# Two norm sums and three PSUM bank orders at the passages of a two-layer backbone

## The chip, the cores and the metric

One core of a Trainium2 chip runs the whole kernel as one program. The metric is the device time of one execution in microseconds (us). Work is spread over five engines that run side by side, each through its own list of instructions in a fixed order: PE (matrix products), DVE (vector engine), ACT (scalar engine), POOL (GpSimd) and SP, which issues the DMAs. An instruction starts when those ahead of it on its engine have gone and the semaphores that it waits for are up.

## The reference, cut to what matters

Two layers work on 640 tokens of width 1024 (128 context tokens and 512 latent ones). Each layer has a mixer (layer 0: mLSTM and HGRN2, layer 1: differential attention) and a SwiGLU feed-forward (FFN). Both add their result to the residual stream x, and each reads x through a norm with a modulation:

```
def _rmsnorm(x, g):
    xf = x.astype(f32)
    return xf * lax.rsqrt(jnp.mean(xf * xf, axis=-1, keepdims=True) + EPS) * g.astype(f32)
```

So each of these passages needs, for every token, the sum over the 1024 channels of x squared, its inverse root r, and x times r times a scale plus a shift. A final norm follows the last layer. All of it is in fp32. A large product is made as three, from a rounded high part and a low part of either operand.

## The kernel before, in words

x lies in SBUF with channels on partitions: eight tiles (k = 0 to 7) of 128 channels, each with 640 tokens in two halves of 320 (HALF; a = 0 and 1). There are three **passages** in the middle, all written by `transition` (L534), and one at the end, `to_output`: T01 from the mixer of layer 0 to its FFN (about 478 to 524 us of the span), T10 from that FFN to the attention (968 to 1020 us), T11 from the attention to the last FFN (1338 to 1390 us), and the output (from 1796 us).

A passage runs thus. The last products of the stage before are added to x, half 0 first, one k after the other (`add_x`, L370, on DVE). `sq_sum` (L480) squares the eight tiles of that half on ACT (L488); POOL adds the squares k = 1 to 5 into `sq` (L490); the squares k = 6 (`s2`) and k = 7 stay as they are, so that the sum is handed on in three parts. `columns` (L549) lets PE add over channels: five groups of 64 tokens, three matmuls with one column each, for the three parts; then DVE adds EPS (`r`, L554), POOL takes the power -1/2 (L555) and DVE spreads r on a diagonal (`dg`, L557). `spread` (L560) multiplies `dg` by ones on PE, so that a PSUM bank `rs` holds r for all partitions. DVE multiplies x by `rs` (L503, tile `hf`), ACT and DVE modulate (L511, L513), the high part `hh` is a cast (L519) and the low part `hl` a subtraction (L525); in these chains the order on DVE is pinned. The adds to x of half 1 run beside this, with `sq_sum` for half 1. `BEFORE` says behind which product of half 1 `columns` and `spread` of half 0 are written.

Then `switch` releases the PSUM banks of the old stage, allocates those of the new, and returns `first`, which makes the first products of the new stage from half 0 (`proj_open`): for T01 and T11 (`to_ffn`) the products u and v and then a second u, for T10 (`to_odd`) two products of q and k and then one of v. `BEHIND` says behind which k of these products PE does `columns` and `spread` for half 1. PE keeps program order within a passage; on the other engines and in the FFN stages a scheduler sets it.

`sq_sum`'s second adds, POOL's own additions of FFN weights (L1283 to L1286) and the power L555 share POOL's list. At T10 a one-row piece of the attention's parameters comes by DMA (`lp`, issued at L1537), and DVE multiplies it at L1540.

In the output, `sq_sum` is called for each half, and `chunk` uses the parts for 128 tokens at a time: means on PE, then transposes and a scaling on DVE and ACT, then the DMA out.

Of the kernel before, what the change touches and what calls it, by code (L numbers as in the profile page):

```python
# [163 lines left out]
def hybrid_kernel(ctx: ExitStack, tc: tile.TileContext, A: dict, O: dict):  # L164
# [316 lines left out]
    def sq_sum(pool, a):  # L481

        t = slice(a * HALF, (a + 1) * HALF)
        sq = pool.tile([P, HALF], F32, tag="nsq", name="sq", bufs=2)
        s2 = pool.tile([P, HALF], F32, tag="ns2", name="s2", bufs=1)
        for k in range(KD):
            dst = {0: sq, SQUARES: s2}.get(k) or pool.tile([P, HALF], F32, tag="ns1", name="s1", bufs=2)
            S.activation(dst, x[:, k, t], AF.Square)  # L488
            if 0 < k < SQUARES:
                G.tensor_tensor(sq, sq, dst, op=ALU.add)  # L490
        return sq, s2, dst

    def norm_out(pool, l, which, a, rs, ks=range(KD), keep=None):

# [44 lines left out]
    def transition(l, which, add, tag0, switch, tag1, nada, ada_bank, extra=0):  # L539
# [7 lines left out]
        def columns(sq, tag):  # L547

            o = bank(tag)  # L549
            for i in range(NC64):  # L550
                for j, part in enumerate(sq):
                    T.matmul(o[0:64, i:i + 1], lhsT=part[:, i * 64:(i + 1) * 64], rhs=mean1, start=j == 0, stop=j == 2)
            r = pool.tile([64, NC64], F32, tag="nr", name="r", bufs=2)
            V.tensor_scalar(r, o[0:64, 0:NC64], EPS, None, op0=ALU.add)  # L554
            G.tensor_tensor(r, r, mhalf[0:64, 0:NC64], op=ALU.pow)  # L555
            dg = pool.tile([64, NC64, 64], F32, tag="ndg", name="dg", bufs=1)
            V.tensor_tensor(dg, ident[0:64, 0:64].unsqueeze(1).to_broadcast([64, NC64, 64]),  # L557
                            r.unsqueeze(2).to_broadcast([64, NC64, 64]), op=ALU.mult)
            return dg
# [774 lines left out]
    def ffn_open(l, behind):  # L1334
# [7 lines left out]
        with tc.issue_after(behind):  # L1342
            w2 = w_cols(A["ffn_w1"][l], P)

        def first(a, between):
            (u, v), t = proj_open(ws, a, between)
            ffn_up(st, 0, u, t)
            ffn_gate(st, 0, v, t)
            ffn_act(st, 0, t)
            (u,), t = proj_open([w2], a, lambda k: between(k + KD))  # L1350
            ffn_up(st, 1, u, t)

        def rest():
# [138 lines left out]
    def to_odd(behind):  # L1492
        ff["st"]["wide"].release()
        ff["st"]["pool"].release()
        psum["p"].release()
        psum_pool(pj=2, s=2, p1=2)
        ff["od"] = tc.alloc_tile_pool(name="od", bufs=1, reuse_waits="tile")
        qk[0] = at_tiles()
        ws = [w_cols(w_in1, j * D, "r") for j in range(2)]
        with tc.issue_after(behind):  # L1500
            wv = w_cols(w_in1, 2 * D)
        ff["vt"] = vt_tile()

        def first(a, between):
            os, t = proj_open(ws, a, between)
            for j in range(2):
                at_evac(j, qk[0][j], a, os[j], t)
            (o,), t = proj_open([wv], a, lambda k: between(k + KD), [bank("s", 2)[:, 0:HALF]])
            S.copy(ff["vt"][:, t], o)

        return first
# [262 lines left out]
    def to_output():  # L1774
        ff["st"]["wide"].release()
        with tc.tile_pool(name="fi", bufs=1, reuse_waits="tile") as fi:
# [13 lines left out]
            def chunk(c):  # L1790
                o = bank("nm")
                for a in range(2):
                    t0, t1 = max(c * P, a * HALF), min((c + 1) * P, (a + 1) * HALF)
                    if t0 < t1:
                        for j, part in enumerate(sqs[a]):
                            T.matmul(o[t0 - c * P:t1 - c * P, 0:1], lhsT=part[:, t0 - a * HALF:t1 - a * HALF],
                                     rhs=mean1, start=j == 0, stop=j == 2)
                V.tensor_scalar(rcol[:, c:c + 1], o[:, 0:1], EPS, None, op0=ALU.add)
                G.tensor_tensor(rcol[:, c:c + 1], rcol[:, c:c + 1], mhalf[:, 0:1], op=ALU.pow)
                for b in range(2):  # L1800
# [58 lines left out]
```

## Time and profile before

| | us |
|---|---|
| median of 3 runs (1825.88 to 1830.09) | 1828.68 |
| the profiled execution | 1829.14 |
| its span in the trace | 1827.4 |
| PE busy in the span | 1751.1 (96%) |
| DVE busy | 1338.0 (73%) |
| ACT busy | 767.4 (42%) |
| POOL busy | 434.2 (24%) |

The span is what the trace covers; the 1.7 us between it and the execution's own time lie around it. In rows of the timeline the first number is the start in us from the span's start, the second the duration of the row (of all its instructions, where it ends in x2 or more), and in square brackets stands how long the engine was idle just before, and who ended that. `nm`, `p`, `pj` and `s` are PSUM tiles, `raw` and `own` are weights as they come in.

### The profile page before, as it was taken

Reading aid. Unit: us, or ns where it says so; the run is one execution under the profiler, and the core shown is the slowest. Engines: PE = TensorE matmul, PEld = TensorE weight load, DVE = VectorE, ACT = ScalarE, POOL = GpSimd, SP = SyncE. Lnnn points to the kernel's source line nnn. Section 1 sums busy time; section 2 is a strip of 40 time slices with the busy share of each in tenths; the row PEclk is TensorE's granted clock in tenths of the full one; section 3 lists DMA queues with packets and bytes.
Section 4 is the critical chain, followed back from the end, with each engine's and each line's share of the span. In section 5 each row is a group of like instructions: output and inputs, shape, how many; then the busy total and the mean of one; then the engine's idle time right before and its main releaser. Section 6 shows DMA issues by size and latency. Waiting matters only on the chain.

```text
span 1827.4 us, 31939 instructions
## 1 busy us (share of the span) xinstructions
PE 1751.1 (96%) x12446; PEld 1673.6 (92%) x12446; DVE 1338.0 (73%) x2778; ACT 767.4 (42%) x1617; POOL 434.2 (24%) x373
## 2 busy tenths in 40 slices
PE   7999999999888999999999899999989999999998
PEld 5788999998778999999998898999978999999998
DVE  5645775668687777777777678667869887887876
ACT  5434343333352333333334466566635333333334
POOL 2100012223313222222212221112131423332312
PEclk9999999999989999999999999999999999999999
DMA  9255222123515344444313121012031322223211
GB/s 310 90 153 169 77 64 64 51 72 99 165 48 172 115 151 127 139 128 136 107 56 101 40 88 44 28 54 76 28 116 58 93 82 81 82 81 93 70 58 58
DMA packets 191818, 174.80 MB, mean 96 GB/s; under 512 B 7506, under 2 KB 176308, under 8 KB 191668
## 3 DMA queue, kind: packets, MB, share of 16 engines
q1 hardware_dynamic: 190404, 172.62, 30.7%
q8 instruction: 99, 1.62, 0.4%
q14 instruction: 51, 0.42, 0.1%
q10 hardware_dynamic: 1264, 0.14, 0.1%
HBM read 167.99 MB, written 4.74 MB: 95 GB/s over the span
## 4 chain that ended last, share of the span: by engine, by line
PE 80%; DVE 11%; ACT 3%; issue 2%; DMA 2%; POOL 1%; ACTq 0%; SPq 0%; POOLq 0%; DVEq 0%
PE pj L187 61%; PE nm L187 8%; PE p L187 6%; PE s L187 2%; DVE wl L318 2%; PE p L192 1%; DVE x L370 1%; ACT wh L317 1%; DVE hl L525 1%; PE pj L192 1%; DMA raw<-in_ffn_w_dram 1%; DVE hh L519 1%; DMA wg<-in_ev_w_in_dram 0%; DVE e L1662 0%; DVE t L1259 0%
## 5 line engine op out<-in xcount | busy, mean ns | idle before, releaser
L187 PE MATMUL pj<-hh,wh 128*128 128x320 f32 x1648 | 526.8, 322 | 20.0 <-DVE hf L503 9.3
L187 PE MATMUL pj<-hh,wl 128*128 128x320 f32 x1648 | 513.7, 312 | 0.6 <-DVE wl L318 0.6
L187 PE MATMUL pj<-hl,wh 128*128 128x320 f32 x1648 | 502.1, 312 | 2.1 <-DVE hl L525 1.9
L187 PEld LDWEIGHTS pj<-hh,wh 128*128 128x128 f32 x1648 | 313.7, 191 | 34.4 <-DVE hf L503 9.6
L187 PEld LDWEIGHTS pj<-hh,wl 128*128 128x128 f32 x1648 | 313.7, 190 | 1.0 <-DVE wl L318 1.0
L187 PEld LDWEIGHTS pj<-hl,wh 128*128 128x128 f32 x1648 | 310.0, 190 | 4.3 <-DVE hl L525 2.4
L187 PE MATMUL pj<-t,wh 128*128 128x320 f32 x960 | 215.8, 310 | 0.0
L317 ACT CAST wh<-raw 128x1024 fp32r<-128x1024 f32 x127 | 132.8, 1050 | 193.1 <-PE pj L187 89.3
L318 DVE TENSOR_TENSOR wl<-raw,wh 128x1024 fp32r<-128x1024 f32 x127 | 158.8, 1252 | 54.0 <-ACT wh L317 44.0
L187 PEld LDWEIGHTS pj<-t,wh 128*128 128x128 f32 x960 | 160.4, 188 | 2.1 <-DVE o L1321 0.8
L187 PE MATMUL pj<-t,wl 128*128 128x320 f32 x480 | 148.4, 309 | 1.5 <-DVE wl L1270 1.5
L1269 ACT CAST wh<-s 128x1024 fp32r<-128x1024 f32 x80 | 84.1, 1051 | 153.1 <-PE pj L187 153.0
L1283 POOL TENSOR_TENSOR s<-raw 128x512 f32<-128x512 f32 x40 | 56.0, 1399 | 331.4 <-DVE wl L1270 317.7
L370 DVE SCALAR_TENSOR_TENSOR x<-nm,g2h,x 128x128 f32<-128x128 f32 (+1 forms) x236 | 93.5, 429 | 49.2 <-PE nm L187 49.0
L370 DVE SCALAR_TENSOR_TENSOR x<-pj,g2h,x 128x128 f32<-128x128 f32 (+2 forms) x292 | 112.0, 431 | 16.2 <-PE pj L187 15.6
L187 PE MATMUL pj<-ah,wh 128*128 128x320 f32 x392 | 122.9, 313 | 0.0
L187 PE MATMUL pj<-al,wh 128*128 128x320 f32 x392 | 121.5, 310 | 0.0
L187 PE MATMUL pj<-ah,wl 128*128 128x320 f32 x392 | 121.4, 310 | 0.0
L1285 POOL TENSOR_TENSOR s<-s,raw 128x512 f32<-128x512 f32 x40 | 67.1, 1678 | 195.7 <-DVE wl L1270 173.3
L1270 DVE TENSOR_TENSOR wl<-s,wh 128x1024 fp32r<-128x1024 f32 x80 | 97.2, 1215 | 8.8 <-ACT wh L1269 8.7
L1269 ACT CAST wh<-raw 128x512 fp32r<-128x512 f32 (+1 forms) x81 | 67.9, 838 | 78.0 <-PE pj L187 77.9
L187 PE MATMUL nm<-al,wh 128*128 128x320 f32 x312 | 95.8, 309 | 1.6 <-DVE al L1385 1.6
(411 smaller groups left out, 3795.4 us busy)
## 6 DMA issues: line engine op xcount, KB each, us to landing
raw<-in_ffn_w_dram SPq DMA_DIRECT2D x132, 512.0 KB
own<-in_ada_w_dram SPq DMA_DIRECT2D x48, 512.0 KB
raw<-in_ev_w_in_dram SPq DMA_DIRECT2D x36, 512.0 KB
raw<-in_ada_w_dram SPq DMA_DIRECT2D x36, 512.0 KB
raw<-in_od_w_in_dram SPq DMA_DIRECT2D x24, 512.0 KB
araw<-in_ada_w_dram SPq DMA_DIRECT2D x12, 512.0 KB
raw<-in_ev_w_out_dram SPq DMA_DIRECT2D x8, 512.0 KB
raw<-in_od_w_out_dram SPq DMA_DIRECT2D x8, 512.0 KB
```

Source lines behind the costliest of these rows:

```text
L187: ins = nc.tensor.matmul(*args, **kw)
L192: ins = nc.tensor.transpose(*args, **kw)
L317: S.copy(wh, raw3)
L318: V.tensor_tensor(wl, raw3, wh.bitcast(F32), op=ALU.subtract)
L370: V.scalar_tensor_tensor(x[:, m, t0:t1], o[:, t0 - a * HALF:t1 - a * HALF], gate[:, m, c:c + 1], x[:, m, t0:t1], op0=ALU.mult, op1=ALU.add)
L519: order(V.tensor_copy(hh[:, k, t], tmps[k]))
L525: order(V.tensor_tensor(hl[:, k, t], tmps[k], hh[:, k, t].bitcast(F32), op=ALU.subtract))
L1269: S.copy(wh, src)
L1270: V.tensor_tensor(wl, src, wh.bitcast(F32), op=ALU.subtract)
L1283: G.tensor_tensor(sa[:, 0], a21, a22, op=ALU.add)
L1285: G.tensor_tensor(sb[:, 0], sa[:, 0], a11, op=ALU.subtract)
```

## The change

`sq_sum` returns one sum. For half 0, POOL still adds k = 1 to 5, and DVE adds k = 7 to `s2` and `s2` to `sq`. For half 1 all seven adds are DVE's. `columns` and `chunk` then have one matmul for a group of tokens in place of three. In `to_ffn` three banks are allocated ahead and handed to the products of half 0 in another order, (1, 2, 0) for layer 0 and (0, 2, 1) for layer 1; in `to_odd` both `s` banks are allocated ahead of the first products.

```diff
@@ sq_sum
             if 0 < k < SQUARES:
-                G.tensor_tensor(sq, sq, dst, op=ALU.add)
-        return sq, s2, dst
+                (V if a else G).tensor_tensor(sq, sq, dst, op=ALU.add)
+            elif k > SQUARES:
+                V.tensor_tensor(s2, s2, dst, op=ALU.add)
+        V.tensor_tensor(sq, sq, s2, op=ALU.add)
+        return sq
@@ columns
-                for j, part in enumerate(sq):
-                    T.matmul(o[0:64, i:i + 1], lhsT=part[:, i * 64:(i + 1) * 64], rhs=mean1, start=j == 0, stop=j == 2)
+                T.matmul(o[0:64, i:i + 1], lhsT=sq[:, i * 64:(i + 1) * 64], rhs=mean1, start=True, stop=True)
@@ to_ffn
+        os = [pj()[:, 0:HALF] for _ in range(3)]
+        os = [os[i] for i in ((1, 2, 0), (0, 2, 1))[l]]
+
         def first(a, between):
-            (u, v), t = proj_open(ws, a, between)
+            (u, v), t = proj_open(ws, a, between, None if a else os[0:2])
...
-            (u,), t = proj_open([w2], a, lambda k: between(k + KD))
+            (u,), t = proj_open([w2], a, lambda k: between(k + KD), None if a else os[2:])
@@ to_odd
+        vs = [bank("s", 2)[:, 0:HALF] for _ in range(2)]
+
...
-            (o,), t = proj_open([wv], a, lambda k: between(k + KD), [bank("s", 2)[:, 0:HALF]])
+            (o,), t = proj_open([wv], a, lambda k: between(k + KD), [vs[a]])
@@ chunk
-                        for j, part in enumerate(sqs[a]):
-                            T.matmul(o[t0 - c * P:t1 - c * P, 0:1], lhsT=part[:, t0 - a * HALF:t1 - a * HALF],
-                                     rhs=mean1, start=j == 0, stop=j == 2)
+                        T.matmul(o[t0 - c * P:t1 - c * P, 0:1], lhsT=sqs[a][:, t0 - a * HALF:t1 - a * HALF],
+                                 rhs=mean1, start=True, stop=True)
```

In the listings below the line numbers of the changed kernel are 2 to 8 higher; a number behind a name tells tiles of one name apart.

DVE at T01, from `r` of half 0 to its first three multiplications by `rs`; `x` is an add to the residual of half 1, `adar` and `g2h` belong to the modulation of a later stage. Before:

```order
L554 TENSOR_SCALAR r<-pj 64x5
L370 SCALAR_TENSOR_TENSOR x<-pj,mod,x 128x320 x2
L453 TENSOR_REDUCE adar<-p_5372 128x4
L557 TENSOR_TENSOR dg<-ident,r 64x320
L471 TENSOR_TENSOR g2h<-adar,v_123 128x4
L370 SCALAR_TENSOR_TENSOR x<-pj,mod,x 128x320
L472 TENSOR_SCALAR g2h<-g2h 128x4
L503 TENSOR_TENSOR hf<-x,pj 128x320 x3
```

Now:

```order
L556 TENSOR_SCALAR r<-pj 64x5
L490 TENSOR_TENSOR sq<-sq,s_5528 128x320
L370 SCALAR_TENSOR_TENSOR x<-pj,mod,x 128x320 x2
L453 TENSOR_REDUCE adar<-p_5374 128x4
L490 TENSOR_TENSOR sq<-sq,s_5531 128x320
L471 TENSOR_TENSOR g2h<-adar,v_123 128x4
L559 TENSOR_TENSOR dg<-ident,r 64x320
L370 SCALAR_TENSOR_TENSOR x<-pj,mod,x 128x320
L490 TENSOR_TENSOR sq<-sq,s_5534 128x320
L472 TENSOR_SCALAR g2h<-g2h 128x4
L506 TENSOR_TENSOR hf<-x,pj 128x320 x3
```

Three adds for half 1 now stand among these rows, and `g2h` stands ahead of `dg`; four more adds stand outside of the piece, one of them ahead of it.

POOL at the same place, from the last add of half 0 to the power for half 1. Before:

```order
L490 TENSOR_TENSOR sq<-sq,s_5533 128x320
L1284 TENSOR_TENSOR s<-raw 128x512
L490 TENSOR_TENSOR sq<-sq,s_5536 128x320
L555 TENSOR_TENSOR r<-r,mhalf 64x5
L1283 TENSOR_TENSOR s<-raw 128x512
L490 TENSOR_TENSOR sq<-sq,s_5539 128x320
L1285 TENSOR_TENSOR s<-s,raw 128x512
L490 TENSOR_TENSOR sq<-sq,s_5542 128x320
L1286 TENSOR_TENSOR s<-raw,s 128x512
```

Now:

```order
L1286 TENSOR_TENSOR s<-raw 128x512
L557 TENSOR_TENSOR r<-r,mhalf 64x5
L1285 TENSOR_TENSOR s<-raw 128x512
L1287 TENSOR_TENSOR s<-s,raw 128x512
L1288 TENSOR_TENSOR s<-raw,s 128x512
```

The adds of half 1 are gone from POOL's list; one of them stood ahead of the power. The four weight sums stay, in the same order.

DVE at the end of T10, from the next to last `wl` (low part of a weight) to `dg` of half 1. Before:

```order
L318 TENSOR_TENSOR wl<-raw,wh 128x1024
L525 TENSOR_TENSOR hl<-hf,hh 128x320
L1540 TENSOR_TENSOR l_11044<-lp 1x128
L1542 TENSOR_REDUCE ls<-l_11044 1x2
L554 TENSOR_SCALAR r<-p_10854 64x5
L1545 SCALAR_TENSOR_TENSOR nl<-ls 1x1
L557 TENSOR_TENSOR dg<-ident,r 64x320
```

Now:

```order
L318 TENSOR_TENSOR wl<-raw,wh 128x1024 x2
L528 TENSOR_TENSOR hl<-hf,hh 128x320
L492 TENSOR_TENSOR s_10744<-s_10744,s_10762 128x320
L528 TENSOR_TENSOR hl<-hf,hh 128x320
L493 TENSOR_TENSOR sq<-sq,s_10744 128x320
L556 TENSOR_SCALAR r<-p_10834 64x5
L1548 TENSOR_TENSOR l_11012<-lp 1x128
L559 TENSOR_TENSOR dg<-ident,r 64x320
```

The last two adds of half 1 stand ahead of `r`; `r` has moved ahead of the instruction that waits for `lp`, and `dg` stands right behind that one.

## Rows read from the trace of the kernel before

**Rows 1.** Windows: busy us and count of PE, PEld, DVE, ACT, POOL; granted clock.

```profile
508.60:512.80 4.20, 4.20 (x16) 4.20 (x17) 3.29 (x8) 1.16 (x2) 0.00 (x0) 0.50 0.16 25
512.90:515.30 2.40, 2.40 (x18) 2.29 (x16) 0.00 (x0) 0.00 (x0) 0.00 (x0) 1.00 0.43 166
```

**Rows 2.** Timeline of PE at T01: start, duration, form, idle time before.

```profile
489.70 0.28 PE L187 MATMUL pj<-mean,sq 128*64 128x1 f32 x2
...
491.54 0.41 PE L187 MATMUL pj<-hh,wh 128*128 128x320 f32 x1
...
496.37 0.77 PE L187 MATMUL pj<-dg,ones 64*128 64x320 f32 x2 [1.70 <-DVE dg L557]
...
508.59 0.63 PE L187 MATMUL pj<-hh,wh 128*128 128x320 f32 x1 [9.31 <-DVE hf L503]
```

**Rows 3.** Timeline of DVE at T01.

```profile
494.67 1.55 DVE L557 TENSOR_TENSOR dg<-ident,r 64x320 f32<-64x320 f32 x1 [0.43 <-POOL r L555]
496.15 2.05 DVE L471 TENSOR_TENSOR g2h<-adar,v 128x4 f32<-128x4 f32 x1
...
498.58 1.68 DVE L472 TENSOR_SCALAR g2h<-g2h 128x4 f32<-128x4 f32 x1
500.18 1.27 DVE L503 TENSOR_TENSOR hf<-x,pj 128x320 f32<-128x320 f32 x3
...
501.91 0.14 DVE L471 TENSOR_TENSOR g2h<-adar,v 128x4 f32<-128x4 f32 x1
```

**Rows 4.** Timeline of POOL at T01.

```profile
492.64 0.87 POOL L490 TENSOR_TENSOR sq<-sq,s 128x320 f32<-128x320 f32 x1
493.47 1.17 POOL L555 TENSOR_TENSOR r<-r,mhalf 64x5 f32<-64x5 f32 x1
494.62 1.25 POOL L1283 TENSOR_TENSOR s<-raw 128x512 f32<-128x512 f32 x1
...
496.90 1.27 POOL L1285 TENSOR_TENSOR s<-s,raw 128x512 f32<-128x512 f32 x1
```

**Rows 5.** One line each: count, duration in ns (least, median, most).

```profile
L490 POOL TENSOR_TENSOR sq<-sq,s x40: 851/876/1100, 482.4 to 1814.8; 128x320 f32<-128x320 f32 x40
```

```profile
L525 DVE TENSOR_TENSOR hl<-hf,hh x24: 473/483/789, 503.0 to 1378.8; 128x320 fp32r<-128x320 f32 x24
```

**Rows 6.** Timeline of PE in the first FFN.

```profile
564.62 0.64 PE L187 MATMUL pj<-own,cpad 128*32 128x256 f32 x8 [2.41 <-DMA own<-in_ada_w_dram]
```

**Rows 7.** Timeline of DVE at T10.

```profile
989.04 1.55 DVE L513 TENSOR_SCALAR hf<-hf,amod,mod 128x128 f32<-128x128 f32 x2
...
996.77 0.63 DVE L513 TENSOR_SCALAR hf<-hf,amod,mod 128x128 f32<-128x128 f32 x2
...
1000.63 0.48 DVE L525 TENSOR_TENSOR hl<-hf,hh 128x320 fp32r<-128x320 f32 x1
1006.29 0.28 DVE L1540 TENSOR_TENSOR l<-lp 1x128 f32<-1x128 f32 x1 [5.18 <-DMA lp<-in_od_lambda_dram]
...
1008.24 0.48 DVE L557 TENSOR_TENSOR dg<-ident,r 64x320 f32<-64x320 f32 x1 [0.94 <-POOL r L555]
```

**Rows 8.** Timeline of PE at T10.

```profile
993.84 0.41 PE L187 MATMUL pj<-hh,wh 128*128 128x320 f32 x1 [3.14 <-DVE x L370]
...
1008.78 1.43 PE L187 MATMUL p<-dg,ones 64*128 64x320 f32 x2 [4.36 <-DVE dg L557]
```

**Rows 9.** Timeline of SP's DMA issues at T10.

```profile
1001.78 0.28 SPq L1537 DMA_DIRECT2D lp<-in_od_lambda_dram  x1
```

**Rows 10.** Timeline of DVE at T11.

```profile
1362.13 1.69 DVE L471 TENSOR_TENSOR g2h<-adar,v 128x4 f32<-128x4 f32 x1
```

**Rows 11.** Timeline of PE at T11.

```profile
1365.14 0.80 PE L187 MATMUL p<-dg,ones 64*128 64x320 f32 x2 [2.62 <-DVE dg L557]
```

**Rows 12.** Timeline of ACT and DVE in the output.

```profile
1815.64 0.82 ACT L488 ACTIVATE s<-x 128x320 f32<-128x320 f32 x2
...
1817.34 0.16 DVE L1798 TENSOR_SCALAR rcol<-nm 128x1 f32<-128x1 f32 x1 [1.86 <-PE nm L187]
```

## The prediction

> **What bounds the kernel now.** I read the page's busy times first, which stand in the table ahead: PE is busy for 96% of the span, so over most of it the time is PE's, and an engine beside it has room. Then the timeline of PE at the three passages and in the output, since there PE stands idle, and each idle time names its releaser. At T01 the columns of half 0 take PE from 489.70 to the next product at 491.54, 1.84 us for fifteen column matmuls (the profile has two records for each); PE then waits 1.70 us for `dg`, makes `rs`, and waits 9.31 us for the first product of the FFN until the last `hf` multiplication [rows 2]. Behind that wait its granted clock is 0.50, 1.2 GHz of 2.4, for 4.2 us in which 16 matmuls were made, against 18 in the next 2.4 us at full clock [rows 1]. Third, the timelines of DVE and POOL at the same place: between `dg` and the first `hf` DVE does little, yet `dg` takes 1.55 us and two operations on 128x4 take 2.05 and 1.68 us, where the same one took 0.14 us at 501.91 [rows 3]; POOL meanwhile goes through its adds, the power and its weight sums without a pause [rows 4]. At T10 PE waits 3.14 us for an add to x and later 4.36 us for `dg` of half 1 [rows 8], which comes behind the landing of `lp` on DVE [rows 7]. At T11 it waits 2.62 us for `dg` [rows 11]. So at the passages the time is set by one chain: columns, r, power, `dg`, spread, `hf`, then the chain on DVE.
>
> **The prices.** An add of the change on POOL has a median of 0.876 us, and twenty go [rows 5]. DVE gains nine adds at each of four places, 36. None of this form is in the trace on DVE; its nearest row is `hl`, the same 128x320 with both inputs in SBUF, with a median of 0.483 us [rows 5]; in an unbroken run, as in the three `hf` that take 1.27 us [rows 3], one costs 0.40 us. I take 0.40 on a chain. As bounds an add costs nothing, where DVE waits anyway, and 1.25 us more where a POOL weight sum of that length holds it up [rows 4]. Of each column place two thirds of the matmuls go: 1.84 x 2/3 = 1.2 us of PE [rows 2].
>
> **T01.** Three things. (1) Half 0: the columns are 1.2 us shorter, so r comes that much earlier. The power no longer stands behind an add (492.64 to 493.51 [rows 4]), but still behind the weight sum that ends where that add began, so it gains only about 0.8 us and ends near 493.85. `dg` then either starts at once or behind L1283, which follows on POOL directly and would end at 495.1; it ended at 496.22, so it gains 0.6 to 1.8 us. Of the two stalled `g2h`, which cost 3.4 us beyond their own length, part goes with two POOL adds in this stretch. I take `hf` to begin 1.5 us earlier than 500.18, from bounds of 0.7 and 2.3. (2) Behind that start three adds (k = 5, k = 7, and the last) stand in the chain that ends with the `hf` for which PE waits: 3 x 0.40 = +1.2. (3) Columns of half 1: -1.2 on PE, which runs without a pause there. Sum -1.5, from -3 to -0.3 by the bounds.
>
> The new order of banks gives nothing here. In the built program the spread of half 0 and the first product stand in the same PSUM bank with either order, so that the first product goes on waiting for the last `hf`, and the 9.31 us only shrink with the chain.
>
> **The FFN behind it.** The scheduler puts some products of the first FFN in another order; the second four of a group on `own` now stand about a dozen matmuls behind the first four, where before eight waited 2.41 us for the DMA [rows 6]. If all were hidden: -2.4; if the wait only moves, or another comes in: 0 to +1. I take -0.5, since a later FFN product may run into the same load.
>
> **T10.** The columns of half 0 give 1.2 us to `rs`. POOL's adds, which stalled the chain, are gone: the modulation took 1.55 us where its like took 0.63 [rows 7], the longest `hl` 0.79 for 0.48 [rows 5], so -1.2 at least. Against it stand six of seven adds ahead of the last `hl`, 6 x 0.40 = +2.4. The last `hl`, at 1000.63 [rows 7], stays where it was, or within a microsecond of it. `lp` is issued behind that, at 1001.78 [rows 9], and DVE takes it at 1006.29 [rows 7], 4.5 us later; I leave this as it is. What is gained is behind it: from the start of the `lp` multiplication to the start of `dg` there were 1.95 us (1008.24 - 1006.29), since r stood behind it and the power behind r; now r is made while `lp` is on its way, and `dg` starts 0.28 us behind. -1.7, and with a last `hl` 0.4 us earlier -2.1. The seventh add stands behind the last `hl`, in the time in which DVE waits for `lp`, so it costs nothing; if that cover went it would be 0.4. Bounds: -3.3 (a last `hl` 1.6 earlier), -0.6 (1.1 later, as the full +2.4 without stalls removed). The wait of 3.14 us goes with the banks, as the first products no longer stand in the bank of the last add to x; but PE only reaches the `hh` casts sooner, and later waits for `dg` as before. I book nothing for it.
>
> **T11.** `dg` stood behind a `g2h` that took 1.69 us [rows 10]. Now r is 1.2 us earlier, POOL's last weight sum starts earlier too, and three adds more stand ahead of `dg`: 2.62 us of waiting [rows 11] become about 1.7, and `rs` comes some 2.1 us earlier. One add then hides under the wait for the spread, two stay in the chain, and I charge a third for holds: +1.2. Columns of half 1: -1.2. Sum -2.1, from -3.5 to 0.
>
> **The output.** The last two squares end at 1816.46, and DVE took the mean at 1817.34 [rows 12]. Two adds, 0.97 us, now stand between: +0.5 for that chunk, as its mean needs fewer matmuls. The two chunks behind it lose four column matmuls each, 4 x 0.12 = 0.5 a chunk. Net -0.4, from -1.5 to +1.5.
>
> **A rule.** Operations of DVE with both inputs in SBUF were long only while POOL was at work: `dg` and `g2h` [rows 3] against POOL's run [rows 4]. The Trainium skill, "SBUF — State Buffer", section "Who interferes with whom", says that a VectorE instruction with two inputs in SBUF contends with a GpSimd instruction that reads SBUF, and that the one that comes first holds the shared ports for its whole length. The trace agrees. By that rule each of the 36 new adds can be held up, and holds up POOL in turn, which speaks against the change: it puts more such instructions on DVE where the weight sums remain.
>
> **The rivals.**
> (a) **Cover only, no change.** T01's `hf` does not start earlier, since the weight sums take the place of POOL's adds: +1.2 - 1.2 = 0. T10 gives the 1.7 behind `lp`. T11 gives its columns less one hold, -0.4, the output -0.4, the FFN nothing: -2.5, 1826.6. For it: POOL has the same four weight sums in the same order. Against it: POOL loses four adds in the same stretch.
> (b) **Slower: the adds are held.** The mechanism is DVE's adds of half 1 waiting for POOL's weight sums and lengthening the chain. T01: +1.2, one hold of 1.25, columns -1.2: +1.3. T10, where POOL has no weight sum, only the adds: +2.8 on the last `hl` and `lp`, less 1.7: +1.1. T11 as T01: +1.3. Output: +0.9 with no column gained back. Sum +4.6, 1833.7. It decides from the point where T01's first `hf` starts no earlier than 500.2 and T10's last `hl` over 1.7 us later than 1000.63. Against it: the stalls at T10 were made by the adds that go. This is where the rule above leads if DVE loses each race.
> (c) **The banks do act at T01**: the first product starts when `hh` is there. PE would then make products while DVE works; some 25 of the matmuls that follow the wait would be made in it, at 0.13 us (2.40 / 18 [rows 1]) 3.3 us: 1819.2. Against it: the placement in the built program.
> (d) **The slow clock goes with the waits.** 16 matmuls took 4.20 us at 0.50 where 18 took 2.40 [rows 1], so this stretch alone is worth 2.1 us; with a second one at T10 or T11 of this size, -4.2 beyond the forecast: 1818.3. Against it: the long waits shrink by 1 to 2 us only.
>
> **How the numbers follow.** The sum: -1.5 - 0.5 - 2.1 - 2.1 - 0.4 = -6.6. The profiled execution took 1829.14 us, 0.46 above the median of 1828.68 and inside the runs' own range: 1829.14 - 6.6 = 1822.5. Chances: forecast 0.44 (1819.5 to 1825), (a) 0.30, (b) 0.10, (c) 0.06, (d) 0.10. 0.2%, about what a measurement of this kernel can tell from no change, is 3.7 us: faster is below 1825.0, slower above 1832.3. The forecast, (c) and (d) are faster, (a) is the same, (b) is slower: 0.60, 0.30, 0.10. The range goes from 1816 (all lower bounds together, -13.7, give 1815.4, which is cut a little) to 1829.5, where (a) ends with the upper bounds of the FFN, +1, and of the output, +1.9 beside its own -0.4. Out of it stay (b) with its 0.10, and some 0.06 at the ends.
>
> **What would show it.** In the profile of the changed kernel: columns of 0.6 us; at T01 the first `hf` about 9 us behind the columns' start in place of 10.5, and PE's wait for the first product still there, near 9 us, ended by `hf`; at T10 `dg` within 0.5 us behind the start of the `lp` multiplication and PE's wait there of about 3 us; at T11 a wait for `dg` under 2 us. The forecast is wrong if the new adds on DVE take over 0.6 us on average, if `lp` lands later than 4.5 us behind its issue, or if the FFN stages, which run on the same products, change by over 2 us between the passages.

## The result, and the profile after

The changed kernel took 1816.76 us in the median (1812.53 to 1819.58, four runs), the kernel before beside it 1829.2 (1825.88 to 1830.09, four runs): a ratio of 0.9934, with an interval of 0.9916 to 0.9951. That is 12.4 us less, faster by more than 0.2%, and about twice the forecast gain of 6.2. It lies inside the predicted range, but only 0.8 us above its lower end (1816), and below the 1819.5 to 1825 that the prediction gave to its forecast alone. The profiled execution of the changed kernel took 1812.53 us, 4.2 below its median. From the page of that execution: busy us, share and instructions of each engine.

```profile
PE 1735.0 (96%) x12302; PEld 1656.6 (91%) x12302; DVE 1351.3 (75%) x2814; ACT 768.1 (42%) x1617; POOL 419.0 (23%) x353
```

POOL has 20 instructions fewer, DVE 36 more, PE 144 fewer, as the diff says. PE's busy time fell by 16.1 us; that counts matmuls at the lower clock at their longer time, so it says little about the end. The idle times and the clock do. The timeline of PE (start, duration, form, idle time before), at T01, T10, T11 and in the output:

```profile
485.56 0.71 PE L187 MATMUL pj<-mean,sq 128*64 128x1 f32 x10
...
492.70 0.77 PE L187 MATMUL pj<-dg,ones 64*128 64x320 f32 x2 [3.37 <-DVE dg L559]
...
503.31 0.64 PE L187 MATMUL pj<-hh,wh 128*128 128x320 f32 x1 [6.98 <-DVE hf L506]
...
995.28 1.20 PE L187 MATMUL p<-mean,sq 128*64 128x1 f32 x10 [4.41 <-DVE sq L493]
...
1000.16 0.80 PE L187 MATMUL p<-dg,ones 64*128 64x320 f32 x2
...
1353.29 0.80 PE L187 MATMUL p<-dg,ones 64*128 64x320 f32 x2 [1.51 <-DVE dg L559]
...
1805.33 1.09 PE L192 MATMUL nm<-ident,xg 128*128 128x128 f32 x8
```

The 1.70 us before the spread at T01 became 3.37, and the 9.31 before the first product 6.98 [rows 2]. At T10 the 4.36 us before the spread of half 1 [rows 8] are gone; in their place PE waits 4.41 us for the last square sum, ahead of the columns. At T11 2.62 us [rows 11] became 1.51. The timeline of DVE: T01, then T10, one add at T11, and the last mean of half 1 in the output:

```profile
488.82 2.19 DVE L490 TENSOR_TENSOR sq<-sq,s 128x320 f32<-128x320 f32 x1
490.94 1.22 DVE L471 TENSOR_TENSOR g2h<-adar,v 128x4 f32<-128x4 f32 x1
492.08 0.48 DVE L559 TENSOR_TENSOR dg<-ident,r 64x320 f32<-64x320 f32 x1
...
494.03 1.27 DVE L506 TENSOR_TENSOR hf<-x,pj 128x320 f32<-128x320 f32 x3
...
994.25 0.48 DVE L528 TENSOR_TENSOR hl<-hf,hh 128x320 fp32r<-128x320 f32 x1
...
996.52 0.15 DVE L556 TENSOR_SCALAR r<-p 64x5 f32<-64x5 f32 x1 [1.38 <-PE p L187]
999.18 0.28 DVE L1548 TENSOR_TENSOR l<-lp 1x128 f32<-1x128 f32 x1 [2.51 <-DMA lp<-in_od_lambda_dram]
999.39 0.47 DVE L559 TENSOR_TENSOR dg<-ident,r 64x320 f32<-64x320 f32 x1
...
1347.56 2.57 DVE L490 TENSOR_TENSOR sq<-sq,s 128x320 f32<-128x320 f32 x1 [0.32 <-ACT s L488]
...
1800.53 0.49 DVE L492 TENSOR_TENSOR s<-s,s 128x320 f32<-128x320 f32 x1 [0.53 <-ACT s L488]
1800.94 0.74 DVE L1815 TENSOR_SCALAR yt<-nm,rcol 128x512 f32<-128x512 f32 x1
1801.60 0.48 DVE L493 TENSOR_TENSOR sq<-sq,s 128x320 f32<-128x320 f32 x1
1802.91 0.16 DVE L1805 TENSOR_SCALAR rcol<-nm 128x1 f32<-128x1 f32 x1 [0.83 <-PE nm L187]
```

The timeline of POOL at T01 and T11 shows what two of these rows ran into:

```profile
489.41 1.26 POOL L1285 TENSOR_TENSOR s<-raw 128x512 f32<-128x512 f32 x1
490.74 1.39 POOL L1287 TENSOR_TENSOR s<-s,raw 128x512 f32<-128x512 f32 x1
...
1347.36 1.17 POOL L557 TENSOR_TENSOR r<-r,mhalf 64x5 f32<-64x5 f32 x1
1348.51 1.26 POOL L1288 TENSOR_TENSOR s<-raw,s 128x512 f32<-128x512 f32 x1
```

At T01 the add at 488.82 ends at 491.01, 0.34 us after POOL's L1285 (489.41 + 1.26), and the `g2h` behind it at 492.16, with L1287. At T11 the add at 1347.56 lasts until 1350.13, through the power and L1288. The issue of `lp` on SP's queue, which at T10 stands behind the last two `raw` loads and one of `rope`:

```profile
994.63 0.28 SPq L1545 DMA_DIRECT2D lp<-in_od_lambda_dram  x1
```

And the windows of T10 (busy us and count of PE, PEld, DVE, ACT, POOL; granted clock; DMA share; GB/s):

```profile
995.20:999.20 4.00, 3.92 (x20) 3.94 (x21) 0.17 (x2) 0.00 (x0) 1.17 (x1) 0.50 0.97 310
1000.20:1004.20 4.00, 4.00 (x25) 3.56 (x25) 2.49 (x8) 2.64 (x7) 0.00 (x0) 1.00 0.02 5
```

The same view of the kernel before, ahead of T10 and behind its wait for `dg`:

```profile
980.40:984.00 3.60, 3.60 (x24) 2.09 (x22) 0.94 (x2) 0.84 (x2) 0.62 (x1) 0.53 0.30 80
1007.80:1011.80 4.00, 3.02 (x8) 2.16 (x9) 1.37 (x3) 0.99 (x4) 0.40 (x1) 0.50 0.00 0
```

PE runs at the lower level, 1.2 GHz, behind its long wait in either kernel. In the changed one that stretch lies while DVE waits for `lp`, and when the spread comes at 1000.16 the clock is back; before, it began with the spread.

**Where the time went, by stage.** Two traces are compared by the start times of the instructions that both have; the difference of these, read in quiet stretches between the passages, steps at each stage. Single profiles of one and the same code differ in such a step by 1 to 2 us and more, so each figure here is a mean over all profiled kernels in which the stage is as before, or as after (the experiments below included; e2, with the new banks alone, counts as before, and e1, with the sums alone, as after). Steps against the first profile of before, in us:

| stage | as before: mean (least to most, kernels) | as after: mean (least to most, kernels) | difference | forecast |
|---|---|---|---|---|
| T01 | -0.1 (-0.4 to 0.2, 7) | -1.5 (-2.1 to -0.7, 4) | -1.4 | -1.5 |
| first FFN | 0.8 (0.0 to 1.4, 7) | 1.5 (1.4 to 1.6, 4) | +0.7 | -0.5 |
| T10 | -0.9 (-1.3 to 0.0, 5) | -6.5 (-7.2 to -5.6, 3) | -5.6 | -2.1 |
| T11 | -0.4 (-2.1 to 1.8, 7) | -2.5 (-4.9 to -1.4, 6) | -2.1 | -2.1 |
| output | 0.4 (-0.1 to 1.0, 5) | -2.5 (-2.9 to -1.7, 7) | -2.9 | -0.4 |
| sum | | | -11.3 | -6.6 |

The sum fits the 12.4 us of the times. The second FFN shows no step (0.0 to 0.2). A step of 4 us before T01, where both programs have the same order, is in the changed kernel's profile and in a second profile of before as well; it belongs to the executions, and is left out.

### The profile page after: what moved, and what is told of

Its sections match the earlier page's. It is cut to its first block, busy times and chain, and to the rows that moved or that the text cites. A ratio compares the mean times of both kernels' runs of the same rounds, so it can differ in the third digit from the quotient of the medians.

```text
span 1810.7 us, 31667 instructions
## 1 busy us (share of the span) xinstructions
PE 1735.0 (96%) x12302; PEld 1656.6 (91%) x12302; DVE 1351.3 (75%) x2814; ACT 768.1 (42%) x1617; POOL 419.0 (23%) x353
## 3 DMA queue, kind: packets, MB, share of 16 engines
HBM read 167.99 MB, written 4.74 MB: 95 GB/s over the span
## 4 chain that ended last, share of the span: by engine, by line
PE 79%; DVE 12%; ACT 3%; issue 3%; DMA 2%; POOL 1%; ACTq 0%; SPq 0%; DVEq 0%; POOLq 0%
PE pj L187 61%; PE nm L187 8%; PE p L187 6%; PE s L187 2%; DVE wl L318 2%; PE p L192 1%; DVE x L370 1%; ACT wh L317 1%; DVE hl L528 1%; PE pj L192 1%; DVE e L1670 1%; DMA wg<-in_ev_w_in_dram 1%; DVE hh L522 0%; DVE sq L490 0%; DVE hf L506 0%
## 5 line engine op out<-in xcount | busy, mean ns | idle before, releaser
L1285 POOL TENSOR_TENSOR s<-raw 128x512 f32<-128x512 f32 x40 | 56.1, 1404 | 332.2 <-DVE wl L1272 330.8
L1287 POOL TENSOR_TENSOR s<-s,raw 128x512 f32<-128x512 f32 x40 | 66.7, 1668 | 197.6 <-DVE wl L1272 181.6
```

Source lines behind the costliest of these rows:

```text
L1285: G.tensor_tensor(sa[:, 0], a21, a22, op=ALU.add)
L1287: G.tensor_tensor(sb[:, 0], sa[:, 0], a11, op=ALU.subtract)
```

## The experiments

The kernels are numbered e1 to e12 (there is no e7). Three ideas were to be told apart: that the sums do it all and the banks nothing; that at T10 the chain of adds, r and `dg` around the load of `lp` sets the time; and that a good part is TensorE's clock, which falls behind a long wait (K, or the clock, in some of the expectations). In e8, e10 and e11 PE makes extra matmuls whose result nobody reads; all of the reference's computation is done in every kernel here. Times are given as a ratio to the kernel before, run beside it, with a 95% interval.

**e1, the sums alone** (the changed kernel, banks put back):

```diff
-        os = [pj()[:, 0:HALF] for _ in range(3)]
-        os = [os[i] for i in ((1, 2, 0), (0, 2, 1))[l]]
-            (u, v), t = proj_open(ws, a, between, None if a else os[0:2])
+            (u, v), t = proj_open(ws, a, between)
...
-            (o,), t = proj_open([wv], a, lambda k: between(k + KD), [vs[a]])
+            (o,), t = proj_open([wv], a, lambda k: between(k + KD), [bank("s", 2)[:, 0:HALF]])
```

> The changed kernel with the bank orders of the kernel before: only the sums of squares are changed. Theory A (the sums carry the gain, the banks nothing): the time of the changed kernel, 1816.8, within 2 us, and a step of -6 to -7 us at T10 when the two timelines are laid side by side. Rival B (the banks let PE make the first products of T10 early, so that its idle time and the slow clock behind it fall into the wait for lp): T10 gives 2 to 3 us less, the first product of T10 waits some 3 us for an add to x again, and the time is 1819.5 to 1821.

1813.2 us, 0.9924 [0.9906, 0.9941]: the whole gain. At T10 the first product waits 2.33 us for an add to x again, and the step there is -7.2 all the same.

**e2, the banks alone** (the kernel before with those lines):

> The kernel before with the new bank orders alone. Theory A: 1829.2 within 2 us; the 3.14 us wait at T10 splits into waits for hh of the same sum, and PE still waits over 4 us for dg of half 1. Rival B: -2 to -4 us, nearly all at T10: 1825 to 1827.

1827.66 us, 1.0008 [0.9995, 1.0022]: nothing. What they do at T10 is seen in PE's timeline of this kernel:

```profile
989.39 0.41 PE L187 MATMUL pj<-hh,wh 128*128 128x320 f32 x1 [0.99 <-DVE hh L519]
...
1004.86 1.43 PE L187 MATMUL p<-dg,ones 64*128 64x320 f32 x2 [4.74 <-DVE dg L557]
```

The 3.14 us for an add to x [rows 8] shrink to waits for `hh` of at most 0.99, and PE then stands 4.74 us before `dg` in place of 4.36. The time was set behind it, and what PE gained it waited off there. At T01 the first product waits 9.30 us for `hf`, as before.

**e3, half 1's adds back on POOL** (the changed kernel):

```diff
             if 0 < k < SQUARES:
-                (V if a else G).tensor_tensor(sq, sq, dst, op=ALU.add)
+                G.tensor_tensor(sq, sq, dst, op=ALU.add)
```

> The changed kernel with the adds k = 1 to 5 of half 1 back on POOL; DVE makes the last two adds of either half, so that there is still one sum and one column matmul a group. Theory P (much of the gain comes from taking POOL's adds away from the DVE chains and from ACT's squares): T10 2 us less gain, the output 2 us less, T01 1 us less: 1821 to 1823. Rival C (the fewer column matmuls and the earlier r give the gain): 1817 to 1818, since DVE has five adds less in each chain.

1820.95 us, 0.9958 [0.9942, 0.9973], 7.7 us below before: of the 12.4, about 4.7 come from the move to DVE, the rest from one sum in place of three parts. The split is rough, as the interval overlaps that of the changed kernel a little. Its T10 gave 3.2 us in place of 6.6, its T11 1.4 in place of 2.5; T01 (-1.2) and the output (-3.2) are as in the changed kernel, against the expectation. The timeline of DVE at T10, then that of PE:

```profile
1005.76 0.28 DVE L1548 TENSOR_TENSOR l<-lp 1x128 f32<-1x128 f32 x1 [5.28 <-DMA lp<-in_od_lambda_dram]
```

```profile
1006.80 1.43 PE L187 MATMUL p<-dg,ones 64*128 64x320 f32 x2 [6.19 <-DVE dg L559]
```

PE gets to the spread early and stands there 6.19 us, and the spread takes 1.43 us as it did before [rows 8]: the adds on POOL don't hold PE up here, but all that is won ahead of `lp` is waited off behind it, and the slow stretch falls behind the wait.

ACT's timeline of the output in this kernel:

```profile
1810.24 0.45 ACT L488 ACTIVATE s<-x 128x320 f32<-128x320 f32 x1
...
1811.05 0.67 ACT L1813 ACTIVATE yt<-nm,rcol 128x512 f32<-128x512 f32 x1
```

The last square stands ahead of that `yt`, though POOL makes half 1's adds; e6 below comes back to it.

**e4 and e5, `lp` loaded ahead of the passage** (the kernel before, then the changed one with the same edit):

```diff
+    lp = sm.tile([P, NB * P], F32, tag="adasb", name="adasb", bufs=2)[0:1].rearrange("p (a d) -> p a d", a=4)
+    Q.dma_start(lp, A["od_lambda"])
     transition(1, 0, last, "nm", to_odd, "p1", ADA_TRANS[1], pj, 4)
...
-    lp = od.tile([1, 4, 64], F32, name="lp")
-    Q.dma_start(lp, A["od_lambda"])
```

> The kernel before, only that lp is loaded some hundred us earlier, into a tile that is free by then, and DVE's multiplication of it no longer waits. Theory L (the landing of lp with r and the power queued behind it set the end of T10 in the kernel before): r is made right behind the columns of half 1 and dg near 1003.9, PE reaches the spread without its 4.36 us wait, and the slow clock behind that wait goes too: -4 to -7 us, 1822 to 1825. Rival M (the chain of adds and hl sets it, lp is hidden beside something else that ends as late): within 1 us of 1829.

Before with `lp` early: 1826.05 us, 0.9983 [0.9971, 0.9995]. The step at T10 is -8.6, 7.4 beyond that of a second profile of before. `dg` now waits only for its own r, in the timeline of DVE, and the spread follows without a wait, in that of PE; the third fence is its window behind that.

```profile
1004.06 0.48 DVE L557 TENSOR_TENSOR dg<-ident,r 64x320 f32<-64x320 f32 x1 [1.28 <-POOL r L555]
```

```profile
1004.76 0.80 PE L187 MATMUL p<-dg,ones 64*128 64x320 f32 x2
```

```profile
1004.80:1008.80 4.00, 4.00 (x25) 3.56 (x25) 2.34 (x7) 2.54 (x6) 0.00 (x0) 1.00 0.48 172
```

The wait of 4.4 us is gone and so is the slow stretch behind it: 25 matmuls in 4 us, against 12 in the like stretch of the second profile of the kernel before, shown further down. The times show less, 3 us of the 7; part of the rest is T11, whose step was 1.8 later in this profile, and what the remainder is stays open.

> The changed kernel with lp loaded some hundred us earlier, as in e4. In the changed kernel's profile dg of half 1 still starts right behind the landing of lp (999.39), but PE has products left until 1000.16 and makes the spread without a wait. Theory A (PE, at its slow clock, ends as late as lp lands, so that lp costs nothing any more): within 0.5 us of the changed kernel at T10, about -12 us to the kernel before. Rival L2 (the landing of lp is still what holds T10): another -2 us, about -14.

The changed kernel with `lp` early: 1817.99 us, 0.9945 [0.9929, 0.996], no better than without. PE's timeline, then a window:

```profile
996.87 1.20 PE L187 MATMUL p<-mean,sq 128*64 128x1 f32 x10 [4.41 <-DVE sq L493]
...
1002.03 1.43 PE L187 MATMUL p<-dg,ones 64*128 64x320 f32 x2
```

```profile
1002.00:1006.00 4.00, 4.00 (x13) 3.11 (x13) 1.43 (x4) 1.91 (x5) 0.00 (x0) 0.50 0.00 0
```

`lp` no longer bounds T10 here. PE waits for DVE's add chain, the same 4.41 us to the hundredth, and the slow stretch behind the wait is longer this time and reaches over the spread. So the step at T10 is -3.9, 2.6 less than in the changed kernel's profile; neither expectation had that. Why the stretch ends later is open.

**e6, one sum in the output only** (the kernel before with a copy `sq_one` of the new `sq_sum`, used by `to_output` alone):

```diff
-                sqs.append(sq_sum(fi, a))
+                sqs.append(sq_one(fi, a))
...
-                        for j, part in enumerate(sqs[a]):
-                            T.matmul(o[t0 - c * P:t1 - c * P, 0:1], lhsT=part[:, t0 - a * HALF:t1 - a * HALF],
-                                     rhs=mean1, start=j == 0, stop=j == 2)
+                        T.matmul(o[t0 - c * P:t1 - c * P, 0:1], lhsT=sqs[a][:, t0 - a * HALF:t1 - a * HALF],
+                                 rhs=mean1, start=True, stop=True)
```

> The kernel before with the new sum of squares in the output alone; the three passages keep three parts. Theory Q (in the output ACT's squares waited for POOL's adds, 0.88 us each, to give back their buffers; DVE's adds of 0.4 us free ACT, and the last square comes 2 us earlier): the output's step is -2 to -4 us and all else stays, about 1823.5. Rival R (the two adds behind the last square take back what the missing column matmuls give, as the prediction had it): -0.4, about 1826.

1823.74 us, 0.998 [0.9971, 0.999], by the ratio -3.7 us, from -5.3 to -1.8; the step in the output is -2.85, the same as in the changed kernel. ACT's timeline of the changed kernel shows how, with one row of the kernel before under it:

```profile
1798.85 0.47 ACT L488 ACTIVATE s<-x 128x320 f32<-128x320 f32 x1
...
1800.03 0.47 ACT L488 ACTIVATE s<-x 128x320 f32<-128x320 f32 x1 [0.25 <-DVE rcol L1805]
...
1800.86 0.67 ACT L1813 ACTIVATE yt<-nm,rcol 128x512 f32<-128x512 f32 x1
```

```profile
1815.07 0.67 ACT L1806 ACTIVATE yt<-nm,rcol 128x512 f32<-128x512 f32 x1
```

The last two squares stand ahead of the `yt` at 1800.86; before, they stand at 1815.64 [rows 12], behind that `yt` at 1815.07. The last square ends 2.2 us earlier against the stage's beginning (1800.50 here; 1816.46 before; the programs are 13.76 us apart there). The reason in the expectation, that DVE's shorter adds free ACT, doesn't hold: in e3 POOL makes these adds, with the same two buffers, and the last square still ends 2.3 us earlier (1810.69, the programs 3.47 us apart).

**e12, more buffers for the squares in the output** (the kernel before, six `s1` in place of two), to see whether the buffers do it:

```diff
-            dst = {0: sq, SQUARES: s2}.get(k) or pool.tile([P, HALF], F32, tag="ns1", name="s1", bufs=2)
+            dst = {0: sq, SQUARES: s2}.get(k) or pool.tile([P, HALF], F32, tag="ns1", name="s1", bufs=n)
...
-                sqs.append(sq_sum(fi, a))
+                sqs.append(sq_sum(fi, a, 6))
```

> The kernel before with six buffers in place of two for the squares of the output; all adds stay on POOL, three parts stay. Theory Q (ACT's squares come late because POOL's adds of 0.88 us hold their two buffers): the squares come earlier and the output's step is -1 to -2 us, a large part of the -2.85 of e6. Rival R2 (the buffers don't matter; what counts is that POOL's power for each chunk stands behind adds in its list, and that a chunk's mean takes six matmuls on PE): within 0.5 us at the output.

1822.3 us in one run (before beside it 1831.63), too few to go by; the step in the output is -1.05. ACT's timeline, then PE's, with the last row of the kernel before:

```profile
1809.02 0.69 ACT L1806 ACTIVATE yt<-nm,rcol 128x512 f32<-128x512 f32 x1 [1.00 <-PE nm L192]
1809.61 0.82 ACT L488 ACTIVATE s<-x 128x320 f32<-128x320 f32 x2
```

```profile
1813.93 1.09 PE L192 MATMUL nm<-ident,xg 128*128 128x128 f32 x8
```

```profile
1820.68 1.95 PE L192 MATMUL nm<-ident,xg 128*128 128x128 f32 x8
```

With buffers enough the two squares still stand behind the `yt`. Of the step 0.9 is the last group of transposes, 1.09 us here and 1.95 in the kernel before, that is the clock. So more buffers alone don't bring the squares forward, and by e3 it isn't the engine of half 1's adds either. What e3, e6 and the changed kernel share is the single sum: two adds on DVE and one matmul in place of three. Which of the two leads the scheduler to the new order on ACT was not tried.

**e8, PE kept busy at T01** (the changed kernel, with 50 unread matmuls ahead of the first product):

```diff
         def first(a, between):
+            if a == 0 and l == 0:
+                o = bank("nm")
+                w = ws[0][0]
+                for i in range(WARM):
+                    T.matmul(o[:, 0:2 * P], lhsT=w[:, 0], rhs=w[:, 2:4].rearrange("p k c -> p (k c)"), start=True, stop=True)
```

> The changed kernel with 50 matmuls of 256 columns on a weight tile, into a PSUM bank that nobody reads, ahead of the first product of the FFN at T01, so that PE is idle for about 1 us in place of 7 there. Theory K (the clock falls because PE stood idle, and the 16 matmuls at 1.2 GHz cost 1.9 us): granted clock 1.00 behind the first product, T01 1.5 to 2 us shorter than in the changed kernel. Rival N (the clock falls there whatever PE did before, or the chain of hh and hl holds PE just as long): 0 to -0.3 us at T01.

1816.74 us, 0.9942 [0.992, 0.9964]: in the times not to be told from the changed kernel. Its PE timeline and the window behind the wait:

```profile
510.08 0.41 PE L188 MATMUL pj<-hh,wh 128*128 128x320 f32 x1 [0.61 <-DVE hf L507]
```

```profile
510.10:514.30 4.20, 4.20 (x29) 4.20 (x30) 3.28 (x8) 1.16 (x2) 0.00 (x0) 1.00 0.12 14
```

29 matmuls in 4.2 us at full clock, where 16 were made before [rows 1]: K holds. The step at T01 is -2.7 against a mean of -1.5, and the one of the first FFN vanishes, as its wait for `own` falls to 0.96 us. These 2.7 us don't appear in the times; T10's step is 1 us smaller here (-5.6), which is part of it.

**e11, PE kept busy at T10** (the kernel before, 27 unread matmuls between the last product and the spread of half 1):

```diff
             if k == after[1]:
+                if not which:
+                    o = bank(tag1)[:, 0:HALF]
+                    for i in range(27):
+                        T.matmul(o, lhsT=hh[:, 0, 0:P], rhs=hh[:, 0, T0], start=True, stop=True)
                 rs = spread(got["dg"], tag1)
```

> The kernel before with 27 matmuls of 320 columns, whose result nobody reads, between the last product and the spread of half 1 at T10, where PE waits 4.4 us for dg. Nothing else starts earlier. Theory K (the slow clock behind this wait is worth as much as the wait itself: 16 products take 4.2 us in place of 2.1): the spread starts when it did, takes 0.8 in place of 1.4 us, granted clock 1.00 behind it, T10 2 to 3 us shorter than in the kernel before. Rival N (the chain of DVE and ACT for half 1 sets the pace behind the spread whatever the clock): T10 within 0.7 us.

1827.26 us, 0.9993 [0.9981, 1.0005]: nothing to be told in the times: 2.5 us, as below, lie inside the interval, and so does nothing at all. PE's timeline and the window from the spread on:

```profile
1001.57 4.12 PE L187 MATMUL p<-hh 128*128 128x320 f32 x27
1006.27 0.77 PE L187 MATMUL p<-dg,ones 64*128 64x320 f32 x2 [0.58 <-DVE dg L557]
```

```profile
1006.30:1010.30 4.00, 4.00 (x24) 3.56 (x25) 2.36 (x7) 2.56 (x6) 0.00 (x0) 1.00 0.00 0
```

The spread starts when it did, relative to the program, and only the clock is different: 24 matmuls in 4 us. From 1001 of the kernel before on, the program gains 2.5 us in this profile. That is the price of the slow stretch at T10, apart from the wait itself.

**The kernel before once more**, one profile:

> The kernel before, profiled once more, to see what a step between two profiles of one and the same program is worth stage by stage. Expected: T01 and T10 agree within 0.5 us, since semaphores of the core's own engines set them; up to T01 and in the first FFN, where PE waits for weights from DMA, up to 4 and 1.5 us; T11 and the output, where weights or the last DMAs take part, 1 to 2 us.

1825.5 us. Its windows ahead of T10 and behind the wait for `dg`:

```profile
976.00:979.60 3.60, 3.60 (x39) 2.71 (x37) 1.10 (x3) 0.81 (x2) 1.17 (x1) 1.00 0.04 11
1004.60:1008.60 4.00, 4.00 (x12) 3.14 (x13) 1.56 (x5) 1.91 (x5) 0.00 (x0) 0.50 0.00 0
```

The second is as in the first profile. The first is not: the slow stretch from 980.40 of the first profile isn't there, which alone is 1.5 us, so that the steps at T10 differ by 1.2 where 0.5 was expected. Behind the wait of 2.41 us for `own` [rows 6] the clock stayed up in the first profile and fell in this one, with the wait equal to the hundredth.

**e9, `lp` early and half 1's adds at T10 on POOL** (the changed kernel; `lp` as in e4, and `sq_sum` takes the engine of these adds as a third argument), **and e10**, the same with the 50 matmuls of e8 at T01:

```diff
-        sq1 = sq_sum(pool, 1)
+        sq1 = sq_sum(pool, 1, None if which else G)
```

> The changed kernel with two edits at T10: lp is loaded early, and the five adds k = 1 to 5 of half 1 are POOL's at this passage alone. In the changed kernel PE waits 4.4 us at T10 for the last add of half 1 on DVE and is then at 1.2 GHz for 5 us or more. Theory D (with lp out of the way DVE's chain of adds is what binds T10, and the idle time brings the slow clock): the wait goes, no stretch at 0.50 behind it, T10 3 to 4 us shorter than in e5 and 1 to 2 us shorter than in the changed kernel: about 1814 to 1816. Rival S (POOL's adds stall DVE's chain again as in the kernel before, and eat the gain): T10 as in e5 or longer, 1817 to 1818.

1817.2 us, 0.9939 [0.9926, 0.9953]. PE's timeline:

```profile
993.50 0.74 PE L187 MATMUL p<-mean,sq 128*64 128x1 f32 x10
...
999.85 1.43 PE L187 MATMUL p<-dg,ones 64*128 64x320 f32 x2 [2.61 <-DVE dg L559]
```

The 4.41 us are gone, a wait of 2.61 and a slow stretch from the spread on have come, and T10 ends where it did: -6.6, 2.7 us better than e5 and no better than the changed kernel.

> e9 together with the matmuls of e8 that keep PE busy at T01. If the two gains add up: T10 as in e9, T01 1.5 to 2 us shorter, 1812 to 1814, faster than both kernels. If the idle time that goes at one passage only lets another wait grow (the weights of the first FFN, on which PE waits some 2.5 us): 1814 to 1816.

1811.97 us (1810.43 to 1815.21), 0.9915 [0.99, 0.993]. It beats the kernel before; its interval overlaps that of the changed kernel, so that it beats this one too is likely and not shown. Its step at T10 is -7.7: the same wait (2.69), but here the spread took 0.77 us, so the clock fell a little later. Its stages T01 and first FFN (-2.6 and 0.1) are as in e8 (-2.7 and 0.0), and yet e10 is some 5 us faster than e9 by the medians, and e8 no faster than the changed kernel; the runs leave open what the 50 matmuls are worth in the times.

## Why the prediction was right in sign and half in size

**What bounds it.** Right in where: the steps stand at the passages and in the output, where PE waits, and the second FFN shows none. That one chain sets the time at each passage is too simple: at T10 the gain is also one of the clock behind the chain, and in the output one of ACT's order.

**Banks: 0.** Right, by e1 and e2, and for both reasons given: at T01 the first product waits for the last `hf` with either order, and at T10 the 3.14 us were waited off before `dg`.

**T01: -1.5.** The size was right (-1.4), the route half wrong. The working had `dg` come 0.6 to 1.8 us sooner, and `hf` 1.5 with it. From the columns to the spread it took 6.67 us before (489.70 to 496.37) and 7.14 after (485.56 to 492.70): the power did come earlier, but `dg` stood behind an add that POOL held up for 2.19 us and a `g2h` of 1.22. The gain came with `dg` and behind it: `dg` itself takes 0.48 in place of 1.55, the second `g2h` 0.16 in place of 1.68, and the first, 2.05 [rows 3], now stands ahead; against that an add of 1.09 has come in. From the spread's start to `hf` it is 1.33 us in place of 3.81. The first `hf` comes 8.47 us behind the columns' start, where 9 was said and 10.5 was before; PE's wait 6.98, where "near 9" was said. Behind it three adds cost 0.9 us up to the last `hf` and the columns of half 1 gave back 0.9 to 1.2, which balance as booked.

**The first FFN: -0.5.** Wrong, within its bounds. The wait for `own` is 2.56 us in the changed kernel, and the step of +0.7 lies inside the befores' own scatter of 0 to 1.4, much of which is the clock: it falls behind this wait in most profiles, ahead of it in e8, e10 and e11 (where the wait is 1.0 to 1.3 us), and in the first profile of before not at all. The scheduler's new order did not hide the wait.

**T10: -2.1.** The mechanism that was named, r made while `lp` is on its way, was right to the tenth; it made a third of the step, and the rest of the gain was luck as far as the working goes. The parts can be read in the changed kernel's profile, whose T10 gives -6.65 (the programs are 4.59 us apart on entry, which is taken off here). The last `hl` starts 1.8 us earlier, of which 1.5 are the slow stretch at 980.40 that the first profile of before had and the second hadn't: so -0.3, where 0 to -0.4 was forecast. From the start of the `lp` multiplication to `dg` 0.21 us in place of 1.95: -1.74, where -1.7 was forecast. Two things were missing. First, `lp` was taken to be issued behind the last `hl`. It stands on SP's queue behind the `raw` loads, which wait for the `wl` that frees their buffer; the second `wl` now comes right behind the first, ahead of the last two `hl`, and `lp` was issued 0.38 us behind the start of the last `hl` in place of 1.15: -0.8. Second, and larger, the clock: -2.6 from the spread to the end of T10. The working said that PE's wait of about 3 us before the spread would stay. It moved ahead of the columns, because the last add, booked at nothing, now releases them, and the slow stretch ran out while `lp` was on its way. e11 measured this term by itself at 2.5, and e4 gave it together with the wait, 7.4. Sum -0.3 - 0.8 - 1.7 - 2.6 = -5.4, with +0.2 from `dg` to the spread -5.2, against -5.6 in the table. So rival (d), "the slow clock goes with the waits", came true at this one place, with 2.6 us where it had worked out 2.1. The stretch at T01 that it started from stayed (16 matmuls in 4.2 us before; the first product behind the wait, at 503.31, takes 0.64 us now and 0.63 before). Its time, 1818.3, is nearer to the measured one than the forecast's 1822.5. Its reason against, that waits shrink by 1 to 2 us only, looked at a wait's length and not at its place.

**T11: -2.1.** Right in sum (-2.1), in a stage whose step scatters by 4 us between kernels with the same code there, so the agreement proves little. The wait for `dg` is 1.51 us, under the 1.7 of the working. Holds came as rival (b) said, adds of 2.57 and 1.39 us, more than the third of an add or so that was charged for them: the long one is 2.1 us over its own length, and PE waited 1.42 us for an add to x behind it. Before, a `g2h` of 1.69 us [rows 10] was held in the same chain and now takes 0.16. These terms can't be told apart by the runs.

**The output: -0.4.** Wrong in size, -2.9, beyond the lower bound of -1.5. The failed step is "the last two squares end at 1816.46": it was taken as fixed, and it came 2.2 us earlier. The two added adds cost more than the 0.5 booked: from the last square's end to `rcol` 2.41 us (1800.50 to 1802.91) in place of 0.88 [rows 12], +1.5, as a `yt` of DVE's stands between them. So `rcol` comes 0.7 us earlier. The column matmuls of the two chunks behind it gave 0.9, as booked, and the last transposes 0.9, by the clock (1.09 us at 1805.33 for 1.95). That last part isn't certain in an execution: in e1 and e9 these transposes took 1.95 us again, and the steps were -1.7 and -1.6. The remaining 0.4 is behind these.

**The rivals.** (a) fell with the T10 and output terms, (c) with e2. (b) fell by its own mark: at T01 the first `hf` starts 2.0 us sooner behind the columns, and at T10 the last `hl` is earlier, not later. Its holds are there, though: adds of 2.19, 1.09, 2.57 and 1.39 us among a median of 0.48. They lift the mean of the 36 adds to 0.63 us, and over 0.6 on average was named as a sign that the forecast is wrong; the sign came, and the kernel is faster all the same, so the mark was badly chosen. The landing of `lp` was at its mark, too (4.55 us behind its issue, over 4.5 named). The rule that (b) leaned on was read too narrowly: the second `g2h` of 1.68 us (L472) [rows 3] has one tile as input, and was long too.

## What to carry to other kernels

Ask of each long wait not only how long it is but what runs behind it: in one profile of the kernel before, a wait of 4.4 us before a spread cost 2.5 us more after it, and 4.41 us in the changed kernel, ahead of work that the wait for `lp` covers, cost almost nothing behind the spread. On an engine that works in order, an instruction that waits for a late small load should stand behind whatever others wait for; at T10 that made `dg` 1.7 us earlier. To issue the load early was worth 7 us in a profile of the kernel before, 3 in its times, and nothing in the changed kernel. And no start time is fixed because the edit doesn't name it: where the change frees buffers or shortens a chain, look at the new order of the engine that fills them, too.

## What was not expected of the hardware

Equal waits have unequal sequels. Behind 2.41 us of waiting for `own` the granted clock over the next 3.2 us was 1.00 in one execution of the kernel before (28 matmuls) and 0.51 in another (21); behind 4.41 us at T10 the spread found it at 1.00 in the changed kernel and at 0.50 in e5. One stage of one profile is therefore uncertain by 1.5 us and more either way, while the median of a few runs tells 4.

An add of DVE that POOL holds up can wait through more than the instruction that POOL is at. The Trainium skill, "SBUF — State Buffer", section "Who interferes with whom", says that of two such instructions the one that comes first holds the ports for its length; by that, if the one that waits counts as first, the add at 1347.56 should have got in when POOL's power ended at 1348.53. It ended at 1350.13, 0.36 us behind the following L1288: it lost twice in a row, and so did the add at 488.82, through the power and L1285. The trace agrees with the lock, and shows that the one that waits isn't always next in turn when POOL's instructions follow each other without a gap. At 1343.32 another add had its turn between two weight sums, after 1.39 us; what decides it stays open. The starts and ends on POOL are rough, so the figures hold to a tenth or two.
